# A hybrid encoder layer on one core: recurrence's values loaded by POOL, fill's weights one piece sooner, decays' rows ahead of sums, gates in quarters, factors a step sooner

## The chip, the core and the metric

The kernel runs on one core of one Trainium2 chip. The metric is the device time of one execution in microseconds; three runs of the kernel before gave 1386.80, 1387.91 and 1392.83 us, so its median is 1387.91 us. The engines are PE (matrix products), DVE and ACT (elementwise work), POOL, and SP, which only starts transfers. Transfers can be started by SP, ACT or POOL; each has its own queue, in which a transfer that waits holds the ones behind it.

## What is computed

One layer of a bidirectional encoder on 1024 rows of width 1024, all in float32:

```python
proj = x @ w_in[l]
(aq, ak, av, gq, gk, gv, gout, lr_f, lr_b, gate_a, gate_g) = jnp.split(proj, IN_SPLITS, axis=-1)
for gi, (win, dil) in enumerate(((128,1), (512,4), (2048,16))):      # mixer A, three groups of 4 heads
    o_g, lse_g = _dilated_group(aq[:, :, hs], ak[:, :, hs], av[:, :, hs], bias, dil, k_side)
mix_w = jax.nn.softmax(jnp.stack(lses, axis=0), axis=0)
y_attn = jnp.sum(mix_w[..., None] * jnp.stack(outs, axis=0), axis=0)
...
b = jnp.cumsum(log_a, axis=3)                                        # mixer B, 4 heads, both directions
chunk_kv = jnp.einsum('bhncd,bhncv->nbhdv', k * jnp.exp(b_last - b), v)
_, s_prev = lax.scan(step, jnp.zeros((B, H, dk, dv), jnp.float32), (decay, chunk_kv))
...
y = sigmoid(gate_a) * (y_attn @ w_attn_branch) + sigmoid(gate_g) * (rmsnorm(o_gla) * silu(gout) @ w_gla_branch)
x = LayerNorm(alpha * x + y @ w_out)
x = LayerNorm(alpha * x + (relu(x @ w_ff1 + b_ff1) ** 2) @ w_ff2 + b_ff2)
```

## The kernel before

Each float32 operand of a product is split into a high and a low part (`halve`: ACT casts the high part, DVE subtracts to get the low part), and `mm3` makes three matmuls of each product (L102, L103, L104). The large projections are computed with sums of input and weight blocks, so DVE adds weights before they are used (L213 to L221, `psum`) and adds products afterwards (`add`, L159).

The places that the change touches, in order of time:

- **The decays' rows.** Early in the program `psteps` runs pieces of 12 matmuls whose products DVE sums at L159 into `fu` and `fcr`. Between them `pre1` (L495) needs two small operands on PE: `lrt`, cast and subtracted by DVE (L470, L471), and `wzr` (L466, L467), from `wz`, which POOL loads.
- **The recurrence** (mixer B, heads 0 to 3). `gv`, 2 MB of values, is loaded from the scratch `gvd` in two halves; `kv` (L549) multiplies them with `kt`, which ACT copies (L541); `states` makes `U` and `S` of the products on DVE (L550 to L569), `out` (L592) uses `S`. Between the heads' steps `fill` puts pieces of other projections on PE, each with its weights: `fetch_raw` loads them (SP), `split` makes the halves, `keep` copies the result to `xb` (L629, ACT) and stores it. `extra` says after which fill a weight is loaded and split. `after_raw` hangs each SP load behind the last one, so SP's order is the order of the code.
- **The steps of `proj`.** A step prepares its weights: two loads of `praw` or `pwhi`, sums on DVE, then halves `pwhi`, `pwlo` (L155 on ACT, L156 on DVE), and 12 matmuls follow three steps later. `yT` and `yB`, two copies of 2 MB each that these steps use later on, are loaded from `xsd` by SP.
- **The units.** While the later steps run, a table hangs other work on them, one unit for each step: the tiles of the attention (`att`, eight for each of the three groups, g = 2, 1, 0) and the gates of mixer B. A tile's parts are `scores` (L893 into the PSUM bank `sc`, read by DVE at L899), `turned` (L917), `values` (L932 into `avp`). For g = 0, `weigh` and `shares` make the factors `f` of the three groups on DVE (L977 to L993), `spread` turns them on PE (L999) into the same bank `sc`, ACT copies them to `fT` and stores them to `fdr`, `loadw` loads them spread out (`W<-fdr`, POOL, held until `fdr` has landed), and `mix` (L953 to L962) multiplies on DVE. `at` gives each tile's unit. A gate is a product and a split on DVE (L1066, L156) and an ACT cast.

Tile's scheduler sets the order within an engine where the code does not (`tc.issue_after`, `behind`) say it.

Of the kernel before, what the change touches and what calls it, by code (L numbers as in the profile page):

```python
# [8 lines left out]
F32 = mybir.dt.float32  # L9
# [63 lines left out]
def build(tc, io):  # L73
# [84 lines left out]
    def add(o, a, b):  # L158
        issued["add"] = V.tensor_tensor(o, a, b, op=OP.add)  # L159
# [577 lines left out]
    del issued["add"]  # L737
# [4 lines left out]
    for i in range(2):  # L742
        issued["raw"] = after_raw(SP.dma_start, gv[:, 4 * i:4 * i + 4], gvd[512 * i:512 * i + 512].rearrange("(t p) f -> p t f", p=128))
    xb_t = ring(P.open("tmp", side="right"), [128, 512], F32, 4, "xb")
    stg = P.open("stg", bufs=2, side="right")
    for h, H in enumerate(heads):
# [6 lines left out]
        if h in (1, 2):  # L753
            load_qk(h + 1)
# [5 lines left out]
        fill(1 if h == 1 else 2)  # L760
        step(H["intra"], 1)
# [90 lines left out]
    def att(g, t):  # L852
# [198 lines left out]
    def gate(hs, part=None):  # L1051
        if hs[0] % 2 == 0 and not part:
            yg.append(xp.tile([128, 2, 4, 512], F32R, tag="act", name=f"yg{hs[0]}"))
        if part:
            pass
        elif hs == (0, 1):
            A.activation(yraw[0][:, :, 0], yraw[0][:, :, 0], AF.Silu)
        else:
            for h, sl, t in gates[hs]:
                A.activation(t[:, 0], t[:, 0], AF.Silu)  # L1060
        for h, sl, t in gates[hs] if part is None else gates[hs][part:part + 1]:
            a, n = 2 * (h % 2) + sl.start // 512, (sl.stop - sl.start) // 512
            o = yg[h // 2][:, :, a:a + n]
            g, y = (t[:, i].rearrange("p (a n) -> p a n", a=n) for i in range(2))
            with behind("add"):
# [952 lines left out]
```

## Time and profile before

| | |
|---|---|
| median of three runs | 1387.91 us |
| the profiled execution | 1391.62 us |
| its span, first to last instruction | 1389.8 us |
| PE busy, share of the span | 1358.5 us, 98% |
| DVE, ACT, POOL busy | 74%, 46%, 10% |
| chain that ended last, by engine | PE 84%, DMA 7%, DVE 4%, ACT 2% |
| mean granted clock of PE | 0.988 of full speed |

PE's idle time and the stretches in which its granted clock is below 1.00 are what is left beside the matmuls. A view of waits groups the idle time of an engine by the instruction that waited and by what released it; a timeline gives each instruction with the idle time in front of it.

### The profile page before, as it was taken

Reading aid. Unit: us, or ns where it says so; the run is one execution under the profiler, and the core shown is the slowest. Engines: PE = TensorE matmul, PEld = TensorE weight load, DVE = VectorE, ACT = ScalarE, POOL = GpSimd, SP = SyncE. Lnnn points to the kernel's source line nnn. Section 1 sums busy time; section 2 is a strip of 40 time slices with the busy share of each in tenths; the row PEclk is TensorE's granted clock in tenths of the full one; section 3 lists DMA queues with packets and bytes.
Section 4 is the critical chain, followed back from the end, with each engine's and each line's share of the span. In section 5 each row is a group of like instructions: output and inputs, shape, how many; then the busy total and the mean of one; then the engine's idle time right before and its main releaser. Section 6 shows DMA issues by size and latency. Waiting matters only on the chain.

```text
span 1389.8 us, 19080 instructions
## 1 busy us (share of the span) xinstructions
PE 1358.5 (98%) x6757; PEld 1125.5 (81%) x6757; DVE 1031.9 (74%) x1782; ACT 640.1 (46%) x1200; POOL 142.0 (10%) x226
## 2 busy tenths in 40 slices
PE   9988989999999999999999999999999999999998
PEld 7967888789777777788888888888888888888886
DVE  7766577366777788767666787887867897786988
ACT  7434665321456544244416655555556533333343
POOL 0000222200344433100001000000000000000001
PEclk9998999999999999999999999999999999999999
DMA  8457654765576677765753565666555965445313
GB/s 307 146 167 243 182 170 159 277 206 185 171 254 224 204 212 212 226 209 195 269 205 132 217 215 173 233 212 219 199 210 166 362 221 165 154 130 160 105 31 122
DMA packets 130212, 272.71 MB, mean 196 GB/s; under 512 B 36677, under 2 KB 48293, under 8 KB 129604
## 3 DMA queue, kind: packets, MB, share of 16 engines
q1 hardware_dynamic: 115060, 235.12, 50.9%
q0 software_dynamic: 11488, 34.88, 7.9%
q10 hardware_dynamic: 3568, 1.49, 0.4%
q8 instruction: 53, 0.87, 0.3%
q14 instruction: 43, 0.35, 0.1%
HBM read 185.57 MB, written 89.01 MB: 198 GB/s over the span
## 4 chain that ended last, share of the span: by engine, by line
PE 84%; DMA 7%; DVE 4%; ACT 2%; issue 1%; SPq 1%; POOL 0%; POOLq 0%; ACTq 0%; DVEq 0%
PE ps L102 18%; PE ps L103 18%; PE ps L104 18%; PE mm L102 6%; PE mm L103 6%; PE mm L104 6%; DMA W<-fdr 1%; DMA fdr<-fT 1%; PE sc L104 1%; PE sc L102 1%; PE sc L103 1%; PE avp L932 1%; DMA pwhi<-in_wfm 1%; PE sc L893 1%; PE tr L917 1%
## 5 line engine op out<-in xcount | busy, mean ns | idle before, releaser
L1390 ACT CAST T<-hp 128x1024 fp32r<-128x1024 f32 x36 | 37.9, 1052 | 109.8 <-PE ps L103 70.3
L1896 POOL TENSOR_TENSOR mv<-mv,mhalf 128x1 f32<-128x1 f32 x8 | 7.0, 877 | 607.3 <-DVE mv L1895 605.8
L103 PE MATMUL ps<-B,B 128*128 128x512 f32 x160 | 62.2, 389 | 0.0
L104 PE MATMUL ps<-B,B 128*128 128x512 f32 x160 | 62.2, 389 | 0.0
L102 PE MATMUL ps<-B,B 128*128 128x512 f32 x160 | 60.9, 390 | 0.5 <-ACT B L1390 0.5
L905 ACT ACTIVATE e<-e,sm 128x256 f32<-128x256 f32 (+2 forms) x96 | 43.3, 453 | 31.4 <-DVE sm L899 31.1
L104 PE MATMUL ps<-T,T 128*128 128x512 f32 x144 | 56.0, 389 | 0.0
L103 PE MATMUL ps<-T,T 128*128 128x512 f32 x144 | 56.0, 389 | 0.0
L102 PE MATMUL ps<-B,T 128*128 128x512 f32 x144 | 56.0, 389 | 0.0
L103 PE MATMUL ps<-B,T 128*128 128x512 f32 x144 | 56.0, 389 | 0.0
L104 PE MATMUL ps<-B,T 128*128 128x512 f32 x144 | 56.0, 389 | 0.0
L102 PE MATMUL ps<-T,T 128*128 128x512 f32 x144 | 56.0, 389 | 0.0
L1391 DVE TENSOR_TENSOR T<-hp,T 128x1024 fp32r<-128x1024 f32 x36 | 44.0, 1222 | 15.2 <-ACT T L1390 15.1
L1791 DVE TENSOR_TENSOR acc<-ps,acc 128x512 f32<-128x512 f32 x68 | 45.7, 688 | 12.7 <-PE ps L104 12.2
L102 PE MATMUL mm<-xB,whi 128*128 128x512 f32 x128 | 51.4, 402 | 0.0
L104 PE MATMUL mm<-xB,wlo 128*128 128x512 f32 x128 | 50.5, 394 | 0.0
L103 PE MATMUL mm<-xB,whi 128*128 128x512 f32 x128 | 50.4, 393 | 0.0
L102 PE MATMUL ps<-T,fraw 128*128 128x512 f32 x128 | 49.6, 390 | 0.4 <-ACT T L1390 0.4
L103 PE MATMUL ps<-T,fraw 128*128 128x512 f32 x128 | 49.8, 389 | 0.0
L104 PE MATMUL ps<-T,fraw 128*128 128x512 f32 x128 | 49.6, 389 | 0.0
L1509 ACT ACTIVATE c<-c,cols 128x512 f32<-128x512 f32 x48 | 34.7, 725 | 27.8 <-DVE c L1570 13.1
L159 DVE TENSOR_TENSOR cr<-cu,mm 128x512 f32<-128x512 f32 x45 | 34.5, 766 | 16.7 <-PE mm L104 16.4
(741 smaller groups left out, 4342.5 us busy)
## 6 DMA issues: line engine op xcount, KB each, us to landing
hdr<-c SPq DMA_DIRECT2D x112, 256.0 KB, 2.6
hp<-hdr SPq DMA_DIRECT2D x56, 512.0 KB, 3.8
spill<-cr SPq DMA_DIRECT2D x48, 256.0 KB, 4.6
raw<-in_wfm SPq DMA_DIRECT2D x17, 512.0 KB, 4.0
praw<-in_wfm SPq DMA_DIRECT2D x16, 512.0 KB, 5.5
pwhi<-in_wfm SPq DMA_DIRECT2D x16, 512.0 KB, 5.1
gate<-spill SPq DMA_DIRECT2D x32, 256.0 KB, 3.1
wa<-in_w SPq DMA_DIRECT2D x16, 512.0 KB, 4.8
```

What stands on the lines that cost most here:

```text
L102: T.matmul(ps, lh, rh, start=first and i == 0, stop=False, skip_group_check=more)
L103: T.matmul(ps, lh, rl, start=False, stop=False, skip_group_check=more)
L104: issued["pe"] = T.matmul(ps, ll, rh, start=False, stop=last and i == n - 1, skip_group_check=more)
L159: issued["add"] = V.tensor_tensor(o, a, b, op=OP.add)
L893: mm = T.matmul(sps[i][:, pr, 0:w], q[ps_, pr], k[ps_, pr, 0:w], start=True, stop=True)
L905: issued["exp"] = A.activation(e, e, AF.Exp, bias=sm[:, h:h + 1], scale=-1.0, accum_out=sm[:, 4 + h:5 + h])
L917: T.transpose(tp[0:hi - lo, pr, j], b["e"][i][:, pr, lo:hi], ident)
L932: return T.matmul(av[64 * i:64 * i + 64, pr], vv[:, h * 64:h * 64 + 64], b["et"][i][p0:p0 + vv.shape[0], pr, j], start=j == pr == 0, stop= ...
L1390: A.copy(o[:, 0], src)
L1391: V.tensor_tensor(o[:, 1], src, o[:, 0].bitcast(F32), op=OP.subtract)
L1509: A.activation(q, src, AF.Relu, bias=cols[:, 2 * j + f:2 * j + f + 1])
L1791: V.tensor_tensor(m, p, m, op=OP.add)
```

## The change

It has six parts, none of which changes an arithmetic operation of the result, only order, queues and the size of pieces.

1. `add` issues behind `issued["decay"]`, the last of `lrt`, `wzr`, and these stand first in the code.
2. `gv` is loaded by POOL (`pool_dma`) and not by SP; the raw weights of the fourth fill piece are loaded earlier on SP.
3. Fill weights are loaded one piece sooner; the third of the attention's value weights has a tile of its own (`vr3`) and is loaded and split first; `load_qk` stands behind the fill.
4. The two 2 MB loads from `xsd` stand behind the raw loads of the first three steps.
5. The gates are made in pieces of 512 columns; those of heads 0 and 1 in four units (35, 37, 39, 41).
6. For g = 0, `shares` comes a unit sooner, `spread` stands right behind `turned` (behind "small", not behind "pe"), and the spacing of the tiles changes.

```diff
     def add(o, a, b):
-        issued["add"] = V.tensor_tensor(o, a, b, op=OP.add)
+        with behind("decay"):
+            issued["add"] = V.tensor_tensor(o, a, b, op=OP.add)
...
-            raws[i] = wp.tile([128, 2, 384], F32, tag="raw", bufs=2, name="raw")
+            raws[i] = (gp.tile([128, 2, 384], F32, name="vr3") if i == 3 else
+                       wp.tile([128, 2, 384], F32, tag="raw", bufs=2, name="raw"))
...
-        if p > 2:
-            extra.setdefault(n - 3, []).append(firsts[p][0])
-    for n, f, i in ((5, v_raw, 0), (5, v_raw, 1), (6, v_split, 0), (6, v_split, 1), (6, v_raw, 3), (6, v_raw, 2),
-                    (7, v_split, 3), (7, v_split, 2)):
+    for p in range(4, NP):
+        n = p if p < 8 else p + 4
+        extra.setdefault({12: 6, 13: 7}.get(n, n - 4), []).append(firsts[p][0])
+    for n, f, i in ((2, v_raw, 3), (4, v_raw, 0), (5, v_raw, 1), (6, v_split, 0), (6, v_raw, 2), (6, v_split, 1),
+                    (7, v_split, 2), (7, v_split, 3)):
...
-    issued["raw"] = after_raw(SP.dma_start, gv[:, 4 * i:4 * i + 4], gvd[512 * i:512 * i + 512].rearrange("(t p) f -> p t f", p=128))
+    pool_dma(gv[:, 4 * i:4 * i + 4], gvd[512 * i:512 * i + 512].rearrange("(t p) f -> p t f", p=128))
...
-        after_raw(SP.dma_start, XQ[nm].bitcast(F32), xsd[i])
...
     for i in range(3):
         steps[i][0]()
+    for i, nm in ((1, "T4"), (0, "B22")):
+        with behind("sp"):
+            issued["sp"] = SP.dma_start(XQ[nm].bitcast(F32), xsd[i])
...
-                with tc.issue_after(issued["pe"].ins):
+                with tc.issue_after(issued["small"].ins):
                     issued["small"] = T.transpose(tp, b["f"][:, 0:3].rearrange("p g h -> p (g h)"), ident)
...
-        for n, part in ((i + 1, 0), (i - 2, 3), (i, 1), (i - 2, 8), (i - 1, 2)):
+        for n, part in ((i + 1, 0), (i - 2, 3), (i, 1), (i - 2, 8), (i - 1, 2), (i - 1, 6)):
...
-    at = [n0 + 2 + (i * 2.7 if i < 8 else 19 + (i - 7) * 1.9 if i < 16 else 36.1 + (i - 16) * 2.4) for i in range(26)]
+    at = [n0 + 2 + (i * 2.7 if i < 8 else 19 + (i - 7) * 1.8 if i < 16 else 35.2 + (i - 16) * 2.7) for i in range(26)]
...
-    for hs, a, bs in (((0, 1), 33, (36, 38)), ((2,), 41, (45, 46)), ((3,), 48, (51, 52))):
+    for hs, a, bs in (((0, 1), 32, (35, 37, 39, 41)), ((2,), 43, (47, 49)), ((3,), 50, (53, 55))):
```

On DVE, where the decays' rows are made (`xr` is the relative bias, `fu` and `fcr` are sums of PE's products). Before:

```order
L450 TENSOR_SCALAR xr_136<-sc 12x512
L159 TENSOR_TENSOR fu_114<-fu_114,mm 128x512
L159 TENSOR_TENSOR fcr_116<-fu_114,mm 128x512
L159 TENSOR_TENSOR fcr_116<-fcr_116,mm 128x512
L470 CAST lrt<-tr 96x512 x2
L471 TENSOR_TENSOR lrt<-tr,lrt 32x512 x2
L466 CAST wzr<-wz 96x512
L467 TENSOR_TENSOR wzr<-wz,wzr 32x512
```

And in the changed kernel, same engine and place:

```order
L451 TENSOR_SCALAR xr_136<-sc 12x512
L469 CAST lrt<-tr 96x512 x2
L470 TENSOR_TENSOR lrt<-tr,lrt 32x512 x2
L471 CAST wzr<-wz 96x512
L472 TENSOR_TENSOR wzr<-wz,wzr 32x512
L160 TENSOR_TENSOR fu_114<-fu_114,mm 128x512
L160 TENSOR_TENSOR fcr_116<-fu_114,mm 128x512
L160 TENSOR_TENSOR fcr_116<-fcr_116,mm 128x512
```

The four instructions on `lrt` and `wzr` moved ahead of the three sums.

On SP, between the early spills and the recurrence, `gv` stands behind the last `fcr` spill before:

```order
L624 DMA raw<-in_wfm 128x1024
L204 DMA spill<-fcr_116 128x512
L204 DMA spill<-fcr_117 128x512
L204 DMA spill<-fcr_118 128x512
L624 DMA gv<-gvd 128x4x512 x2
L624 DMA raw<-in_wfm 128x1024
```

On POOL in the changed kernel the load of `gv` is the next transfer after `wz`, ahead of the first `upk` of a fill piece:

```order
L164 DMA wz<-in_wz 96x512
L473 MEMSET rmask 128x1024
L474 MEMSET rmask 64x8
L475 MEMSET rmask 64x8
L164 DMA gv<-gvd 128x4x512 x2
L164 DMA upk<-xb_1095 128x512
```

So `gv` moved from SP's queue to POOL's.

On PE, in a tile of g = 0, the turning of the factors stands after twelve matmuls of a step before (the rows of these matmuls between are left out here by starting at the last two):

```order
L103 MATMUL mm<-xT_96,pwlo 128x512
L104 MATMUL mm<-xT_96,pwlo 128x512
L999 MATMUL sc<-ident,f_2464 12x128
L102 MATMUL mm<-yT_2396,pwlo 128x512
L103 MATMUL mm<-yT_2396,pwlo 128x512
```

In the changed kernel it follows the tile's own scores and transposes at once:

```order
L902 MATMUL sc<-ak_2449,aq_2446 128x256 x4
L926 MATMUL tr<-ident,e_2455 128x128 x4
L926 MATMUL tr<-ident,e_2456 128x128 x4
L1008 MATMUL sc<-ident,f_2464 12x128
L102 MATMUL mm<-xT_96,pwlo 128x512
```

It moved up by twelve matmuls, to right behind `tr`.

## Rows read from the trace of the kernel before

**Rows 1.** The view of waits of PE over the whole span. Columns: the instruction that waited, what released it, us in total, times, longest.

```profile
PE tr L549 <- DMA gv<-gvd: 4.9, 2, 2.9
PE sc L495 <- DVE wzr L467: 4.6, 1, 4.6
PE mm L102 <- ACT xb L629: 3.2, 1, 3.2
PE mm L104 <- DVE pwhi L156: 2.7, 1, 2.7
PE sc L999 <- DVE f L993: 2.3, 3, 1.4
PE mm L102 <- DVE cr L159: 1.5, 2, 1.1
PE sc L102 <- ACT pwlo L155: 1.4, 1, 1.4
PE av L592 <- DVE S L569: 1.3, 1, 1.3
```

**Rows 2.** The view by windows, the five windows of 25 us in which the granted clock is below 1.00. Columns: window, its length, busy us and instructions of PE, PEld, DVE, ACT, POOL, then the mean granted clock, the DMA share, GB/s.

```profile
75.00:100.00 25.00, 20.45 (x76) 16.01 (x76) 17.07 (x21) 10.23 (x15) 0.00 (x0) 0.86 0.40 114
100.00:125.00 25.00, 19.60 (x92) 16.01 (x91) 12.64 (x21) 7.55 (x11) 1.50 (x4) 0.80 0.74 245
...
175.00:200.00 25.00, 21.74 (x136) 20.38 (x137) 16.58 (x20) 12.79 (x39) 6.62 (x10) 0.93 0.60 196
...
275.00:300.00 25.00, 23.35 (x97) 19.03 (x97) 16.90 (x22) 4.58 (x7) 0.73 (x1) 0.93 0.63 184
...
400.00:425.00 25.00, 22.34 (x117) 17.10 (x117) 19.59 (x51) 14.70 (x37) 10.24 (x17) 0.93 0.70 216
```

**Rows 3.** PE's timeline between 80 and 125 us. Columns: start, us, engine, line, operation, out<-in, count, and in brackets the idle time in front of it with its releaser.

```profile
80.46 1.19 PE L495 MATMUL sc<-lrt,wzr 96*128 96x512 f32 x2 [4.55 <-DVE wzr L467]
...
97.74 0.50 PE L102 MATMUL tr<-xB,swlo 128*128 128x512 f32 x1
...
114.72 2.05 PE L549 MATMUL tr<-gv,kt 128*128 128x128 f32 x8 [2.86 <-DMA gv<-gvd]
...
121.46 0.63 PE L102 MATMUL mm<-xB,whi 128*128 128x512 f32 x1
...
124.44 0.39 PE L103 MATMUL mm<-xB,whi 128*128 128x512 f32 x1
124.67 0.40 PE L104 MATMUL mm<-xB,wlo 128*128 128x512 f32 x1
```

**Rows 4.** DVE's timeline between 75 and 98 us, same columns.

```profile
75.94 0.69 DVE L159 TENSOR_TENSOR fcr<-fcr,mm 128x512 f32<-128x512 f32 x1 [2.06 <-PE mm L104]
...
79.63 0.68 DVE L467 TENSOR_TENSOR wzr<-wz,wzr 32x512 fp32r<-32x512 f32 x1
...
89.70 0.69 DVE L159 TENSOR_TENSOR fcr<-fu,mm 128x512 f32<-128x512 f32 x1 [0.72 <-PE mm L104]
...
97.00 0.68 DVE L159 TENSOR_TENSOR fcr<-fu,tr 128x512 f32<-128x512 f32 x1
```

**Rows 5.** The view of transfers between 60 and 125 us, two of its issues. Columns: out<-in, queue, count, KB each, median us from issue to landing. POOL issued `wz` at 65.81.

```profile
gv<-gvd SPq DMA_DIRECT2D x2, 1024.0 KB, 9.7
...
wz<-in_wz POOLq DMA_DIRECT2D x1, 192.0 KB, 7.8
```

**Rows 6.** SP's timeline and POOL's, the issue of `gv` and the next transfer that POOL issues after `wz`.

```profile
108.54 0.99 SPq L624 DMA_DIRECT2D gv<-gvd  x2
...
111.37 1.10 POOL L163 DMA_DIRECT2D upk<-xb  x2 [43.54 <-ACT xb L629]
```

**Rows 7.** ACT's timeline around 111 us.

```profile
110.48 1.07 ACT L629 COPY xb<-mm 128x512 f32<-128x512 f32 x2 [4.24 <-DMA spill<-fcr]
111.44 1.09 ACT L541 COPY kt<-tr 128x512 f32<-128x512 f32 x2
```

**Rows 8.** ACT's timeline at 163 us, and PE's at 189 us.

```profile
163.52 0.84 ACT L155 CAST wv<-raw 128x768 fp32r<-128x768 f32 x1 [4.87 <-DMA raw<-in_wtv]
...
189.03 0.51 PE L102 MATMUL mm<-whi,xB 128*128 128x384 f32 x1 [3.21 <-ACT xb L629]
```

**Rows 9.** SP's timeline, the second weight load of the third step, issued behind the two loads from `xsd`; and DVE's timeline, the sum that waits for it.

```profile
257.80 0.33 SPq L190 DMA_DIRECT2D pwhi<-in_wfm  x1
...
272.07 0.69 DVE L213 TENSOR_TENSOR psum<-pwhi 128x512 f32<-128x512 f32 x1 [5.57 <-DMA pwhi<-in_wfm]
```

**Rows 10.** DVE's timeline at 407 us, a half of a gate and the low half of a step's weights behind it.

```profile
406.62 1.25 DVE L156 TENSOR_TENSOR yg<-yraw,yg 128x1024 fp32r<-128x1024 f32 x1
407.75 0.72 DVE L156 TENSOR_TENSOR pwhi<-praw,pwhi 128x512 fp32r<-128x512 f32 x1
```

**Rows 11.** PE's timeline, the matmul that follows the transposes L917 in two tiles of g = 0.

```profile
496.57 0.48 PE L102 MATMUL mm<-xT,pwhi 128*128 128x512 f32 x1
...
505.47 0.48 PE L102 MATMUL mm<-xT,pwlo 128*128 128x512 f32 x1
```

**Rows 12.** DVE's timeline in the same two tiles, the second of the four readings of the scores, and one product with the loaded factors in a late tile.

```profile
496.20 0.42 DVE L899 CUSTOM_DVE_ANT_0 e<-sc,strip 128x256 f32<-128x256 f32 x1
...
505.87 0.42 DVE L899 CUSTOM_DVE_ANT_0 e<-sc,strip 128x256 f32<-128x256 f32 x1
...
583.69 0.42 DVE L953 TENSOR_TENSOR W<-avp,W 128x256 f32<-128x256 f32 x1 [3.72 <-DMA W<-fdr]
```

More of the change, by code (lines that the diff above doesn't have):

```diff
@@ L465, in build @@
     pool_dma(wz, io["wz"])
-    V.tensor_copy(wzr, wz)
-    V.tensor_tensor(wzr[64:96], wz[64:96], wzr[64:96].bitcast(F32), op=OP.subtract)
     for i in range(2):
@@ L471, in build @@
         V.tensor_tensor(lrt[32:64, sl], lp[i][32:64], lrt[32:64, sl].bitcast(F32), op=OP.subtract)
+    V.tensor_copy(wzr, wz)
+    issued["decay"] = V.tensor_tensor(wzr[64:96], wz[64:96], wzr[64:96].bitcast(F32), op=OP.subtract)
     G.memset(rmask, 1.0)
@@ L694, in build @@
         extra.setdefault(n - 2, []).append(firsts[p][1])
-        if p > 2:
-            extra.setdefault(n - 3, []).append(firsts[p][0])
-    for n, f, i in ((5, v_raw, 0), (5, v_raw, 1), (6, v_split, 0), (6, v_split, 1), (6, v_raw, 3), (6, v_raw, 2),
-                    (7, v_split, 3), (7, v_split, 2)):
+    for p in range(4, NP):
[3 more added lines that the diff above has]
+                    (7, v_split, 2), (7, v_split, 3)):
         extra.setdefault(n, []).append(lambda f=f, i=i: f(i))
+    extra[6].sort(key=lambda f: f is firsts[8][0])
+    extra[7].sort(key=lambda f: f is firsts[9][0])
     count = itertools.count()
@@ L736, in build @@
                 firsts[1][1]()
-    del issued["add"]
+            firsts[3][0]()
+            issued["sp"] = issued["raw"]
+    del issued["add"], issued["decay"]
     issued["raw"] = issued["sp"]
@@ L752, in build @@
         step(H["intra"], 0)
-        if h in (1, 2):
-            load_qk(h + 1)
         step(H["kv"], 0)
@@ L760, in build @@
         fill(1 if h == 1 else 2)
+        if h in (1, 2):
+            load_qk(h + 1)
         step(H["intra"], 1)
@@ L1049, in gate_load, with gate @@
             pool_dma(t[:, 1], yodr[h, :, sl])
-    def gate(hs, part=None):
-        if hs[0] % 2 == 0 and not part:
+    def gate(hs, part):
+        if hs[0] % 2 == 0 and part == 0:
             yg.append(xp.tile([128, 2, 4, 512], F32R, tag="act", name=f"yg{hs[0]}"))
-        if part:
-            pass
-        elif hs == (0, 1):
+        if part == 0 and hs == (0, 1):
             A.activation(yraw[0][:, :, 0], yraw[0][:, :, 0], AF.Silu)
-        else:
+        elif part == 0:
             for h, sl, t in gates[hs]:
                 A.activation(t[:, 0], t[:, 0], AF.Silu)
[L1061 to L1065, printed above, removed]
-                V.tensor_tensor(y, y, g, op=OP.mult)
-                halve(o[:, 0], o[:, 1], y)
+        n = 2 if hs == (0, 1) else 1
+        h, sl, t = gates[hs][part // n]
+        q = part % n
+        g, y = (t[:, i, 512 * q:512 * q + 512] for i in range(2))
+        o = yg[h // 2][:, :, 2 * (h % 2) + sl.start // 512 + q]
+        with behind("add"):
+            V.tensor_tensor(y, y, g, op=OP.mult)
+            halve(o[:, 0], o[:, 1], y)
     vs = ap_.tile([128, 2, 768], F32, tag="strip1", name="vs")
@@ L1157, in build @@
         units.setdefault(n, []).append(lambda i=i: visit(i))
-        for k, part, later in ((i - 1, 6, 1), (i, 4, 1), (i, 5, 2), (i - 1, 7, 1), (i - 2, 9, 1)):
-            if 0 <= k < 24 and (later == 1 or k > 15):
+        for k, part, later in ((i, 4, 1), (i, 5, 1), (i - 1, 7, 1), (i - 2, 9, 1)):
+            if 0 <= k < 24:
                 units.setdefault(n + later, []).append(lambda k=k, part=part: tiles[k][part]())
```

## Prediction, made before the changed kernel ran

> **What bounds the kernel now.** PE does. I read the shares of the engines first: PE is busy nearly throughout, and the chain that ended last is PE for most of its length. So only what shortens PE's stops, or what they do to its clock, can pay; DVE, ACT and the queues count where PE waits for them. Then I read the waits of PE, to see how few there are: eight entries hold 22.4 us [rows 1]. Then the windows of 25 us, to see what a stop costs beyond itself: the granted clock is below 1.00 in five windows only, and each holds one of the long stops [rows 1, 2]. A clock of 1.00 is 2.4 GHz and half of it 1.2 GHz; a mean of c over 25 us means 2 x (1 - c) x 25 us at the low level, and PE loses at most half of that: 3.5, 5.0, and three times 1.75, together 13.75 us [rows 2]. The matmuls confirm the two levels: seven pitches from 121.46 to 124.44 are 0.426 us each, the next is 0.23 [rows 3]. Stops of up to 1.4 us were followed by no such window [rows 1, 2]; 1.4 plus a second of 0.2 just behind it was. So a stop of some 1.6 us or more costs about 1.75 us on top. Last I read the timelines around each stop, to see what ends the wait and what stands next in line.
>
> **Part 1, decays' rows.** PE stopped 4.55 us at 80.46 for `wzr`, which DVE made only after the sum at 75.94, itself held by PE [rows 3, 4]. In the new order the four small instructions stand ahead of the sums. What then holds `wzr` is its load: issued at 65.81, 7.8 us to landing, so 73.6 [rows 5], plus the cast (0.4) and subtraction of 0.68 [rows 4]: 74.7, before PE arrives at 80.46 - 4.55 = 75.9. The stop goes, and with it most of the first window's clock loss: I take 3.0 of the 3.5 [rows 2]. Gain 7.55. The sums now stand behind a load; if it landed 1.2 us later, PE would wait again.
>
> **What is late next.** The decays' chain (ACT, then DVE's scans) starts only 4.55 us earlier plus 0.3 for its own products at full clock. DVE's idle 0.72 at 89.70, a wait for PE, vanishes too [rows 4]. So DVE's sum at 97.00 ends at 97.7 - 5.5 = 92.2, while PE reaches the matmul behind it, which it started at 97.74 with hardly a wait, at 97.74 - 7.55 = 90.2 [rows 3, 4]. A new stop of 2.0 us, at which the clock may fall (half a chance of 1.75 to 2: 1.0). A known stop of 0.5 just behind it, for the next sum, is absorbed.
>
> **Part 2, gv by POOL.** SP issued `gv` at 108.54, behind three spills that wait for their sums; it took 9.7 us [rows 5, 6], and PE stopped twice, 4.9 us in all [rows 1], with up to 5.0 of clock behind it [rows 2]; I take 3.8, since part of that time PE stood still. POOL has nothing to issue for 43 us before 111.37 [rows 6]. In its queue `gv` waits only for the last reader of the memory that it takes, which stands ahead of the matmul at 97.74 [rows 3]. Issued as late as that, moved up with PE to 90.2, it lands at 99.9. PE wants it at 114.72 - 2.86 = 111.86 [rows 3], less 7.55 and the 0.5, plus the new 2.0: 105.8. Slack 5.9 us. Gain 8.7 and the 0.5.
>
> Then the other operand is late: ACT's copies `kt` at 111.44, done at 112.5, stand behind copies that waited 4.24 us for a spill's landing [rows 7]. That chain is DVE's and moves with it, 5.5 us: 107.0 against 105.8, a stop of 1.2 to 1.4, too short for the clock by the rule above. So parts 1 and 2 give 7.55 + 9.2 - 2.0 - 1.0 - 1.4 = 12.4 us; without any new stop 16.8, with the clock falling at both of them and twice the stops about 8.
>
> The POOL rows show the descriptors' price: two issues of 128 rows each take 1.10 us together [rows 6], and each half of `gv` has 512. The Trainium skill speaks against this move: "SBUF — State Buffer", section "SBUF: two separate sides", says that a transfer issued by GpSimd needs that engine to write its descriptors, that it cannot while DVE runs certain two-port operations, and advises to issue from SP or ACT. By that rule the issue would stretch while DVE works at 80 to 90 us; POOL does nothing between 75 and 100 us here [rows 2], so no row shows it. It is a rival below; the slack of 5.9 us is what it must exceed.
>
> **Part 3, fill's weights.** At 163.52 ACT had waited 4.87 us for a load of the value weights, and everything behind it on ACT and DVE, with it `S` and the copies `xb`, was late by that much [rows 8]. PE's stops of 1.3 for `S` and 3.2 for `xb` follow [rows 1, 8], and 1.75 of clock [rows 2]: 6.3 in all. In the new order this weight has memory of its own, is loaded after the third fill, and is split early; the chain of `S` starts when PE's products are there. The later `q` and `k` loads move behind one or two fills, and stay well ahead of their use. I take 5.5: the early cast now stands ahead of keep copies on ACT, and a wait of half a microsecond there is likely. Bounds 3 and 6.3.
>
> **Part 4, xsd.** The load at 257.80 stood behind 4 MB and reached DVE at 272.07 after 14.3 us, where DVE had stood 5.57 us [rows 9]. PE's stop is 1.4 plus 0.2, and 1.75 of clock [rows 1, 2]: 3.35. With the 4 MB behind it, the load takes less; only 1.6 us less is needed. What was ahead is now later: the 4 MB land at worst the same 14.3 us after their issue, about 273, and their first reader stands 36 matmuls (8 us at 0.23) behind the matmul that stopped near 276. About 10 us of cover. I take 3; bounds 1.4 and 3.4.
>
> **Part 5, gates.** DVE's gate halves of 1.25 us stood ahead of a weights' half at 407.75 [rows 10]; PE stopped 2.7 us, and 1.75 of clock [rows 1, 2]: 4.4. In the new order half of the gate's work comes behind these weights, two products and two subtractions of 1.25 us each in halves, that is 2.5 us of DVE work less ahead of them. The 2.7 goes nearly whole; I take 3.5, bounds 1 and 4.4, since quarters in later units may press elsewhere.
>
> **Part 6, factors.** It removes the three waits for `f`, 2.3 us, and likely the two for `cr`, 1.5, since the factors' loads, for which DVE stood 3.72 us at 583.69 [rows 12], start sooner [rows 1]. But the turned factors go into the bank of the scores, and now PE must wait, right behind its transposes, until DVE has read that bank twice. In one tile the second reading ended at 496.62, PE was there at 496.57; in another, 506.29 against 505.47 [rows 11, 12]. So a stop of 0.05 to 0.8 in each of eight tiles. From the new order on DVE I count four with nothing ahead (0.1 each), three with three or four 0.6-us rows ahead (0.4 to 0.5), and the last tile, whose factors themselves end behind six such rows (some 1.7): 3.7. Net 0; bounds -6 (all stops at 0.8, two more at 2 us with a fall of the clock) and +3.5.
>
> **Sum.** 12.4 + 5.5 + 3.0 + 3.5 + 0 = 24.4 us. The profiled execution took 1391.6 (span 1389.8), so 1367 there. It stands 3.7 above the median of the runs shown, which no stop explains; the same stops are in both, so from 1387.9 I forecast **1363 us**.
>
> **The rivals.**
> - The gaps close whole: all bounds at their best, 16.8 + 6.3 + 3.4 + 4.4 + 3.5 = 34.4, so 1353.5. For it: every removed wait has a named cause. Against it: DVE's chain at 97 us moves less than PE. 8%.
> - The chain of DVE takes over: the new stops for `fcr` and `kt` are twice as long and each drops the clock, and part 3 gives 3: 8 + 3 + 3 + 3.5 = 17.5, so 1370. For it: DVE is continuous from 89.7 to 97.7 but for the one wait [rows 4]. 20%.
> - POOL's descriptors: `gv` comes over 5.9 us later than I think and the stop with its clock stays: 8.7 are given back, and the 1.4 for `kt` with them not paid: 24.4 - 7.3 = 17.1, 1371. For it: four times the rows of any issue seen here, while DVE is busy. Against: the issues seen are short [rows 6]. 6%. (The Trainium skill, "SBUF — State Buffer", section "SBUF: two separate sides", is the rule for it.)
> - Slower: the wait for the scores' bank is long in every tile. If DVE has two more rows ahead of the readings, each of eight stops is 0.8 + 1.2 = 2.0, and the clock falls each time, 1.75: 30 us, less the 3.7 counted: 24.4 - 26.3, so 1390; with three rows more, 2.6 + 1.75 each, 1395. It decides from 24.4 / 8 = 3.1 us a tile beyond what I counted. For it: three rows of 0.6 us are enough to get there. Against: four tiles have nothing ahead. 2%.
> - The change does little: the new orders of parts 3 to 6 only move waits, and part 1 and 2 give 8: 1380. 7%.
> - My forecast, 1357 to 1367: 57%.
>
> **How the numbers follow.** 1363 is the likeliest case. The range 1355 to 1377 leaves out most of the first and the last two or three. A measurement of this kernel tells about 0.5% (6.9 us) from no change, so faster means below 1381: forecast, first three rivals and most of the last, 0.94; same 0.04; slower 0.02.
>
> **What would show it.** No waits of PE for `wzr`, `gv`, `pwhi` at 400 us or `xb` at 189; a wait for `fcr` of about 2 us near 90, and for `kt` of 1.4 near 105; `gv` issued by POOL at 80 to 90 and landed 10 us later; windows with a clock below 1.00 only near 90; `sc` at the factors' turning waiting for L908, 0.1 to 0.8 us each, some 1.7 in the last. Wrong would be a stop at `gv`, at the value weights or of over 2 us at each tile.

## The result, and the profile after

The changed kernel takes **1370.24 us** (median of four runs, 1369.64 to 1375.09) where the kernel before takes 1387.36 in the same runs: a ratio of 0.988, 95% interval 0.984 to 0.991. The forecast was 1363, its range 1355 to 1377: right side, inside the range, and 7 us too fast. It lies outside the 1357 to 1367 that the prediction kept for its forecast, on the 1370 of its second rival. The profiled execution took 1369.64 us (span 1367.9).

PE's waits, the longest (columns as in [rows 1]):

```profile
PE sc L1008 <- DVE sm L908: 5.3, 4, 3.8
PE av L102 <- DVE fcr L160: 4.1, 1, 4.1
PE sc L1008 <- DVE f L1002: 1.8, 1, 1.8
PE sc L902 <- DMA ak<-spill: 1.7, 2, 1.3
PE tr L102 <- DVE fcr L160: 1.5, 1, 1.5
...
PE mm L102 <- ACT xb L630: 0.4, 1, 0.4
```

The waits for `gv`, `wzr`, `pwhi`, `pwlo` and `S` of [rows 1] are gone, and that for `xb` has shrunk from 3.2 to 0.4 us. The longest of the new ones are 5.3 us for the bank of the scores (`sm` L908) and 4.1 for `fcr`; the wait for `ak`, 0.4 us before, is 1.7 now and stood in no term of the prediction. Windows of 25 us, columns as in [rows 2]:

```profile
75.00:100.00 25.00, 19.39 (x79) 14.96 (x79) 16.92 (x19) 10.91 (x15) 1.55 (x2) 0.95 0.77 217
100.00:125.00 25.00, 25.00 (x127) 20.50 (x128) 16.53 (x28) 13.04 (x17) 2.06 (x5) 0.92 0.61 189
175.00:200.00 25.00, 25.00 (x169) 23.07 (x168) 20.18 (x31) 15.85 (x25) 6.74 (x14) 1.00 0.67 209
275.00:300.00 25.00, 25.00 (x142) 24.42 (x141) 17.75 (x24) 8.12 (x12) 2.17 (x3) 1.00 0.70 222
400.00:425.00 25.00, 24.55 (x158) 19.25 (x157) 18.86 (x52) 15.74 (x40) 11.57 (x18) 1.00 0.75 248
525.00:550.00 25.00, 20.76 (x114) 16.10 (x114) 20.43 (x66) 9.29 (x28) 7.50 (x13) 0.93 0.70 184
```

Three of the five clock losses of [rows 2] are gone and two are smaller; the one at 525 us is new. Now the place of the 4.1 us, first DVE and PE by their timelines:

```profile
73.43 0.68 DVE L472 TENSOR_TENSOR wzr<-wz,wzr 32x512 fp32r<-32x512 f32 x1
...
96.46 1.23 DVE L530 TENSOR_TENSOR k<-k,ex 128x1024 f32<-128x1024 f32 x1 [5.34 <-DMA k<-spill]
97.60 0.68 DVE L160 TENSOR_TENSOR fcr<-fcr,av 128x512 f32<-128x512 f32 x1
```

```profile
98.34 0.79 PE L102 MATMUL av<-xB,swlo 128*128 128x512 f32 x1 [4.10 <-DVE fcr L160]
98.93 0.63 PE L103 MATMUL av<-xB,swlo 128*128 128x512 f32 x1
...
104.05 0.43 PE L103 MATMUL mm<-xB,whi 128*128 128x512 f32 x1
```

The name behind PE's wait is a sum that takes 0.68 us; DVE's row ahead of it shows the cause: `k<-k,ex` stood 5.34 us for the landing of `k`, and the sum stood behind it. From 98.93 to 104.05 there are 12 pitches of 0.427 us, the low clock, where 0.23 is the full one [rows 3]: 2.4 us more. Now POOL's timeline, and the view of transfers between 60 and 112 us (columns as in [rows 5]):

```profile
78.98 0.79 POOL L164 DMA_DIRECT2D gv<-gvd  x1 [11.81 <-PE mm L104]
85.42 0.76 POOL L164 DMA_DIRECT2D gv<-gvd  x1 [5.66 <-issue]
```

```profile
gv<-gvd POOLq DMA_DIRECT2D x2, 1024.0 KB, 6.2
...
q<-spill SPq DMA_DIRECT2D x4, 256.0 KB, 9.0
k<-spill SPq DMA_DIRECT2D x4, 256.0 KB, 8.0
```

The second half of `gv` goes out at 85.42, when the first has landed, and moves beside SP's `q` and `k` (issued from 86.38 on), of which `q` took 5.1 us before and takes 9.0 now. In windows of 5 us the DMA share, the last column but one, is above 1 in these ten microseconds:

```profile
90.00:95.00 5.00, 3.06 (x12) 2.18 (x12) 1.13 (x2) 3.48 (x5) 0.00 (x0) 1.00 1.05 251
95.00:100.00 5.00, 1.66 (x4) 1.37 (x5) 3.54 (x4) 0.00 (x0) 0.00 (x0) 0.73 1.06 229
```

The other stop is in a tile of g = 0 (DVE's and PE's timelines; between the two DVE rows stand, among others, eleven rows of 0.68 us, sums and weights of the steps of `proj`):

```profile
519.46 0.42 DVE L962 TENSOR_TENSOR W<-avp,W 128x256 f32<-128x256 f32 x1 [2.91 <-DMA W<-fdr]
...
529.86 0.42 DVE L908 CUSTOM_DVE_ANT_0 e<-sc,strip 128x256 f32<-128x256 f32 x1
```

```profile
530.68 0.30 PE L1008 MATMUL sc<-ident,f 128*12 128x128 f32 x1 [3.77 <-DVE sm L908]
```

DVE had waited 2.91 us for the factors to come back from memory, then worked off the rows that had gathered, and only then read the scores. PE had ended its transposes at 526.9. In the eight tiles of g = 0 PE waited, in order, 0, 0.19, 0, 0.83, 0, 3.77 and 0.47 us for the bank, and in the last 1.76 us for the factors `f` themselves.

### The profile page after: what moved, and what is told of

It reads as the page before. It is cut to its first block, busy times and chain, and to the rows that moved or that the text cites. A ratio compares the mean times of both kernels' runs of the same rounds, so it can differ in the third digit from the quotient of the medians.

```text
span 1367.9 us, 19100 instructions
## 1 busy us (share of the span) xinstructions
PE 1346.4 (98%) x6757; PEld 1119.6 (82%) x6757; DVE 1033.7 (76%) x1786; ACT 637.6 (47%) x1200; POOL 143.5 (10%) x228
## 4 chain that ended last, share of the span: by engine, by line
PE 59%; DVE 1%; ACT 1%; DMA 1%; issue 0%; POOL 0%; ACTq 0%; DVEq 0%; POOLq 0%
PE ps L102 18%; PE ps L103 18%; PE ps L104 18%; PE mm L102 1%; PE mm L103 1%; PE mm L104 1%; ACT xr L1417 1%; DMA W<-fdr 0%; PE ps L1414 0%; DMA fdr<-fT 0%; PE ps L1925 0%; DVE cr L160 0%; DVE W L970 0%; PE ps L1921 0%; ACT T L1398 0%
## 5 line engine op out<-in xcount | busy, mean ns | idle before, releaser
L1398 ACT CAST B<-hp 128x1024 fp32r<-128x1024 f32 x20 | 21.0, 1052 | 55.4 <-PE ps L103 48.1
```

Source lines behind the costliest of these rows:

```text
L1398: A.copy(o[:, 0], src)
```

## The experiments

Two theories stood at the start. A: the 24.4 us on record were missed because of part 6, whose waits for the scores' bank give back more than was counted. B: `gv` on POOL takes the transfers that `k` needs, and makes the 4.10 us stop. The rival to each: DVE is late anyway, and the lateness moves on to the next thing whatever is undone.

Each was run against the kernel before again (1385.7 to 1386.5 us in these runs). A price "by medians" is against the changed kernel's 1370.24, which rests on four runs; its ratio's interval is 5 us wide to either side, so of those prices only the order of size counts. Prices "in the stretch" are read from the traces: PE's time from one of these marks to the next, the first product with `S` of head 0, the first scores (`sc<-ak,aq`), and the first product of `T` and `fraw`, behind the attention. In the changed kernel these three rows are:

```profile
131.65 0.39 PE L593 MATMUL av<-S,q 128*128 128x128 f32 x2
...
325.48 0.72 PE L902 MATMUL sc<-ak,aq 64*128 64x128 f32 x8
...
758.80 0.74 PE L102 MATMUL ps<-T,fraw 128*128 128x512 f32 x2 [0.41 <-ACT T L1398]
```

How far such a price can be trusted is shown by the stretches that an edit did not touch. From `S` to the first scores the ten profiles with parts 3 and 4 lie between 193.81 and 193.90 us. From there to `T` the eight with parts 5 and 6 lie between 433.23 and 435.86. Up to `S` one profile, in which only part 5 was undone, is 4.9 us longer than the changed kernel's. So a difference of 2 or 3 us ahead of `S` or behind the first scores, read from one profile, may be that of two executions.

**The kernel before, a second profile.** No edit.

> The kernel before as it is, for a second profile. Theory P (its first profiled execution, 1391.62 where the median is 1387, lost more clock than a usual one, and the terms worked out from it are too large by that): the second profile is nearer 1387, with the same stops within 1 us and a granted clock above 0.988. Rival (all of its executions have that clock, and a profiled one is always some 4 us longer): about 1391 again at 0.988, and the stops of the first.

1385.78 us, median of 12; its profiled execution took 1386.75 (span 1384.9, clock 0.990), 4.9 us less than the first. The same marks, and the stop at 275 us:

```profile
140.03 0.39 PE L592 MATMUL av<-S,q 128*128 128x128 f32 x2
...
275.20 0.50 PE L102 MATMUL sc<-xT,pwlo 128*128 128x512 f32 x1 [1.43 <-ACT pwlo L155]
276.15 0.50 PE L104 MATMUL sc<-xT,pwlo 128*128 128x512 f32 x1 [0.21 <-DVE pwlo L156]
...
342.07 0.71 PE L893 MATMUL sc<-ak,aq 64*128 64x128 f32 x8
...
774.12 0.74 PE L102 MATMUL ps<-T,fraw 128*128 128x512 f32 x2 [0.41 <-ACT T L1390]
```

```profile
275.00:300.00 25.00, 24.59 (x114) 20.92 (x115) 17.86 (x23) 5.07 (x9) 0.73 (x1) 1.00 0.72 213
```

Theory P holds. The stop of 1.43 and 0.21 us is the same as in the first profile, to the hundredth, and this time no low clock followed it (1.00 here, 0.93 in [rows 2]): 1.75 us. The waits for `cr` were 0.3 us here and 1.5 in [rows 1]: 1.2.

**gv on SP again** (part 2 undone for `gv` alone).

```diff
-    pool_dma(gv[:, 4 * i:4 * i + 4], gvd[512 * i:512 * i + 512].rearrange("(t p) f -> p t f", p=128))
+    issued["raw"] = after_raw(SP.dma_start, gv[:, 4 * i:4 * i + 4], gvd[512 * i:512 * i + 512].rearrange("(t p) f -> p t f", p=128))
```

> The changed kernel with gv loaded by SP again, behind the last spills. Theory B, gv's 2 MB on POOL's queue delay the k loads that DVE waits for: k lands 3 us or more sooner, the 4.1 us wait for fcr falls to 1 or less with its low clock (about 2), and the waits for gv come back with their clock (8.7): 1370 + 8.7 - 6 = 1373. Rival, k is late for its own issue: the wait for fcr stays at 4 and 1379.

1375.69 us (ratio 0.990 to 0.993), 2.7 above theory B's sum. DVE's and PE's timelines:

```profile
92.85 1.23 DVE L530 TENSOR_TENSOR k<-k,ex 128x1024 f32<-128x1024 f32 x1 [1.81 <-DMA k<-spill]
```

```profile
94.73 0.50 PE L102 MATMUL av<-xB,swlo 128*128 128x512 f32 x1 [0.58 <-DVE fcr L160]
...
108.44 1.13 PE L550 MATMUL tr<-gv,kt 128*128 128x128 f32 x8 [3.20 <-DMA gv<-gvd]
```

With `gv` out of the way `k` is there 3.6 us sooner and the 4.10 us are 0.58. So `gv` made `k` late, and theory B holds for the stop. In return `gv`'s own two stops are 3.20 and 3.28 us, 6.5 in all and more than the 4.9 of [rows 1]. Part 2 is worth 2.6 us in its stretch, 5.4 by medians.

**gv on POOL, but only once k's factor is made** (one column of `ex` copied into `gv`, so that its load waits).

```diff
     for i in range(2):
+        G.tensor_copy(gv[:, 4 * i, 0:1], qk["ex", 0][:, 0:1])
+    for i in range(2):
         pool_dma(gv[:, 4 * i:4 * i + 4], gvd[512 * i:512 * i + 512].rearrange("(t p) f -> p t f", p=128))
```

> The changed kernel with gv still on POOL, but held until ACT has made ex (near 92 us), by a copy of one column of ex into gv that the load then overwrites. Theory B: k lands near 94 and the wait for fcr falls from 4.1 to about 1 with its low clock; gv still comes in time or under 1.5 us late: 1365 to 1367. Rival, k is late anyway: the wait for fcr stays at 4 and gv is late as well, 1371 to 1375.

1374.05 us, in the rival's range and not in theory B's. POOL's and PE's timelines:

```profile
92.94 0.79 POOL L164 DMA_DIRECT2D gv<-gvd  x1 [0.46 <-DMA k<-spill]
102.48 0.77 POOL L164 DMA_DIRECT2D gv<-gvd  x1 [8.74 <-DMA spill<-fcr]
```

```profile
107.83 2.05 PE L551 MATMUL tr<-gv,kt 128*128 128x128 f32 x8 [2.28 <-issue]
```

The stop for `fcr` fell to 0.82 us, as theory B has it, and two others came instead: 2.28 us at 107.83 and 1.92 at 111.80. Only the second is `gv`'s. At the first, the first half of `gv` had landed long before (92.94 and 9.2 us); what came just ahead of PE's row is ACT's copy `kt` at 107.13, behind a copy that had waited for raw weights. Again the second half of `gv` went out only when the first had landed (9.2 us here).

**The sum ahead of k's product** on DVE.

```diff
-            V.tensor_tensor(qk["k", h], qk["k", h], ex, op=OP.mult)
+            kx = lambda: V.tensor_tensor(qk["k", h], qk["k", h], ex, op=OP.mult)
+            if h:
+                kx()
...
+        if n == 7:
+            with tc.issue_after(issued["add"].ins):
+                for f in qk["late"]:
+                    f()
```

(`late` holds the products of `k` and `q` of head 0.)

> Only edit against the changed kernel: head 0's product k*ex stands one row later on VectorE, behind the sum of fcr and av instead of ahead of it; loads and queues stay. Theory B (the 4.10 us stop of TensorE at 98.34 is k's late landing, passed on only because the sum stands behind the product that waits for k): the stop falls to 0.5 to 1.0 and the granted clock of 95 to 105 us stays near full, so 3.2 us of stop and some 2 us of clock go: 1365 by the changed kernel's 1370.2. Rival (k itself is what is late, and the next thing that needs it takes the stop over): a stop of 2 to 4 us at the transposes of k or at the next sum, 1369 to 1371.

1372.58 us (1369.55 to 1375.65). DVE's, SP's, ACT's and PE's timelines:

```profile
99.03 1.22 DVE L95 TENSOR_TENSOR wlo<-raw,whi 128x1024 fp32r<-128x1024 f32 x1
```

```profile
100.28 0.33 SPq L631 DMA_DIRECT2D raw<-in_wfm  x1
```

```profile
106.27 1.04 ACT L93 CAST whi<-raw 128x1024 fp32r<-128x1024 f32 x1 [3.00 <-DMA raw<-in_wfm]
```

```profile
109.23 3.78 PE L556 MATMUL tr<-gv,kt 128*128 128x128 f32 x16 [4.39 <-ACT kt L548]
```

My theory fell. The 4.10 us stop went entirely, and a 4.39 us stop for `kt` came 11 us later: ACT's copies `kt` stand behind a cast that waits for raw weights. These are late because `k` is: SP issued their load at 100.28, just as DVE's row `wlo`, which reads the weights loaded before, had ended (99.03 and 1.22 us), and `wlo` stands behind the product of `k` at 96.75, which had waited 4.98 us for `k`. In the changed kernel the two rows stand at 99.34 and 100.58, as late, but there PE had already stood still at the sum. So `k`'s lateness is handed on to whatever stands behind its product, as the rival has it. The mark at `S` stands at 132.14, 0.5 us later than in the changed kernel.

**k first on SP**, head 1's `q` and `k` behind the raw weights.

```diff
-        for nm, base in (("q", 0), ("k", 2)):
+        for nm, base in (("k", 2), ("q", 0)):
...
-            for h in range(2):
-                load_qk(h)
+            load_qk(0)
             firsts[2][0]()
...
             firsts[3][0]()
+            load_qk(1)
```

> Only edit against the changed kernel: k goes out ahead of q on SP, and head 1's q and k (1 MB) stand behind the raw weights and not ahead of them. Theory B (k is late because the second half of gv and 2 MB of q and k share the transfer engines from 86 to 97 us): k goes out 1.3 us sooner and shares with less, so the product k*ex starts at 93 to 94.5 and not 96.46; TensorE's 4.10 us stop for fcr falls to 1 to 2.5, the raw weights land sooner too, and no stop takes its place: 1365 to 1367 by the changed kernel's 1370.2. Rival (what is late moves on, as it did when the sum was put ahead of the product): the first stop shrinks and TensorE stops 2 us or more at kt, gv or the next weights: 1369 to 1372.

1375.61 us (1372.11 to 1376.4), 3.6 above even the rival's upper end. ACT's and PE's timelines:

```profile
110.92 1.07 ACT L630 COPY xb<-mm 128x512 f32<-128x512 f32 x2 [4.66 <-DMA spill<-fcr]
```

```profile
98.10 0.50 PE L102 MATMUL av<-xB,swlo 128*128 128x512 f32 x1 [2.81 <-DVE fcr L160]
...
112.54 3.62 PE L550 MATMUL tr<-gv,kt 128*128 128x128 f32 x16 [2.40 <-ACT kt L542]
```

`k` went out 0.9 us sooner than in the changed kernel (86.81), but its product began only 0.24 us sooner (96.22). The first stop shrank by 1.3 us and `kt` stopped PE for 2.40: head 1's loads now stood ahead of two spills of `fcr` on SP, for whose landing the copies `xb` wait, and `kt` stands behind these. `S` is 2.7 us later than in the changed kernel. Whatever went first, something of this stretch came late.

**Part 1 undone** (`lrt`, `wzr` behind the sums; the core of it).

```diff
     def add(o, a, b):
-        with behind("decay"):
-            issued["add"] = V.tensor_tensor(o, a, b, op=OP.add)
+        issued["add"] = V.tensor_tensor(o, a, b, op=OP.add)
```

> The changed kernel with part 1 put back (the rows of lrt and wzr behind the sums). By the prediction's terms, 7.55 less the 2.0 and 1.0 that it counted for what is late next, part 1 is worth 4.5: 1374.7, with a stop of 4.5 us for wzr near 80 us and no 4.10 us stop for fcr. Rival (the 4.10 stop behind it, which is a transfer's, stays as long as it is, because gv's loads move with TensorE): 1377 to 1378.

1378.4 us (1376.24 to 1379.92). PE's timeline:

```profile
105.24 0.79 PE L102 MATMUL av<-xB,swlo 128*128 128x512 f32 x1 [5.65 <-DVE fcr L159]
```

The stop of 4.55 us for `wzr` is back, at 80.16, and the rival is right: the stop for `fcr` stays, and is longer. So it was not PE's earlier arrival that made it, as the prediction had it. Part 1 is worth 6.9 us in its stretch.

**Part 3 undone** (the fill's weights, `vr3` and the place of `load_qk` as before; the core of it).

```diff
-            raws[i] = (gp.tile([128, 2, 384], F32, name="vr3") if i == 3 else
-                       wp.tile([128, 2, 384], F32, tag="raw", bufs=2, name="raw"))
+            raws[i] = wp.tile([128, 2, 384], F32, tag="raw", bufs=2, name="raw")
...
+        if p > 2:
+            extra.setdefault(n - 3, []).append(firsts[p][0])
```

> The changed kernel with part 3 put back (the fill's weights, the third value weight's own tile and the places of the later q and k loads as before). By the prediction's term 5.5: 1375.7, with stops for xb and S back near 150 and 180 us. Rival (its bounds, 3 and 6.3 us): 1373 or 1376.5.

1381.4 us (median of 12), more than either said. In its stretch the price is 5.2 us (the marks are 133.06, 332.13 and 766.22), the term on record being 5.5. The stops of [rows 1] return, that for `xb` at half its length (PE's timeline):

```profile
167.09 0.61 PE L593 MATMUL av<-S,q 128*128 128x128 f32 x2 [1.36 <-DVE S L570]
...
181.06 0.45 PE L102 MATMUL mm<-whi,xB 128*128 128x384 f32 x1 [1.80 <-ACT xb L630]
```

Of the rest, 1.4 us lie ahead of `S`, 0.8 between the first scores and `T`, and 1.3 behind `T`; the profiled execution took 1378.41 us, the least of the twelve. Why the others are longer was not settled.

**Part 4 undone.**

```diff
+        after_raw(SP.dma_start, XQ[nm].bitcast(F32), xsd[i])
...
-    for i, nm in ((1, "T4"), (0, "B22")):
-        with behind("sp"):
-            issued["sp"] = SP.dma_start(XQ[nm].bitcast(F32), xsd[i])
```

> The changed kernel with part 4 put back (the two rows of xsd that the decays need go out ahead of the raw loads again, from where they were). By the prediction's term part 4 is worth 3.0 us: 1373. Rival (the stop it removes returns elsewhere, as it did for part 6): 1370 to 1371.

1373.73 us (1373.39 to 1374.83), as the term on record has it: 3.5 more by medians, 1.85 us in the stretch from `S` to the first scores. The stop is back, 1.29 and 0.21 us at 261.14 and 262.08 for `pwlo`, and no low clock followed.

**Part 5 undone** (gates in halves again; the table of their units).

```diff
-    for hs, a, bs in (((0, 1), 32, (35, 37, 39, 41)), ((2,), 43, (47, 49)), ((3,), 50, (53, 55))):
+    for hs, a, bs in (((0, 1), 33, (36, 38)), ((2,), 41, (45, 46)), ((3,), 48, (51, 52))):
```

> The changed kernel with part 5 put back (the gates in halves, at their old places in the list). By the prediction's term part 5 is worth 3.5 us, stops at the gates of 2 us and more return between 365 and 420 us: 1373.7. Rival (most of the old stop was not the gates' size): 1370 to 1371.

1376.57 us (1371.71 to 1381.73), above both forecasts; the profiled execution took 1381.4 and is 6.0 us longer from the first scores to `T`. PE's timeline:

```profile
395.81 0.70 PE L104 MATMUL mm<-xT,pwhi 128*128 128x512 f32 x1 [2.67 <-DVE pwhi L156]
```

The order of [rows 10] is back (at 392.03 and 393.16), and the stop of 2.7 us of [rows 1], with a clock of 0.93 from 375 to 400 us, and 1.5 and 0.4 us more for `et` besides; PE no longer waits for `ak`. Not all of the 6.0 us is the part's: behind the stop for the scores' bank, 3.53 us here and 3.77 in the changed kernel, the clock from 525 to 550 us was 0.86 and not 0.93, which is 1.75. That leaves some 4.2.

Up to `S`, which this edit does not touch, the same execution lost 4.9 us more than the changed kernel's (136.58 against 131.65). DVE's and PE's timelines:

```profile
75.15 0.42 DVE L471 CAST wzr<-wz 96x512 fp32r<-96x512 f32 x1 [4.83 <-DMA wz<-in_wz]
```

```profile
103.13 0.79 PE L102 MATMUL av<-xB,swlo 128*128 128x512 f32 x1 [6.75 <-DVE fcr L160]
```

`wz`, issued at 65.47, took 9.7 us to land, where it took 7.8 in the changed kernel. PE waited 0.88 us for `wzr` and 0.70 for a sum, its clock was 0.85 and 0.81 in the two windows of 5 us from 75 on, and the stop for `fcr` was 6.75 us. It is what the prediction warned of in part 1, sums that stand behind a load.

**Part 6 undone**, and **only its turning put back**.

```diff
-                with tc.issue_after(issued["small"].ins):
+                with tc.issue_after(issued["pe"].ins):
...
-        for n, part in ((i + 1, 0), (i - 2, 3), (i, 1), (i - 2, 8), (i - 1, 2), (i - 1, 6)):
+        for n, part in ((i + 1, 0), (i - 2, 3), (i, 1), (i - 2, 8), (i - 1, 2)):
...
-    at = [n0 + 2 + (i * 2.7 if i < 8 else 19 + (i - 7) * 1.8 if i < 16 else 35.2 + (i - 16) * 2.7) for i in range(26)]
+    at = [n0 + 2 + (i * 2.7 if i < 8 else 19 + (i - 7) * 1.9 if i < 16 else 36.1 + (i - 16) * 2.4) for i in range(26)]
```

(The whole part has this and the unit of `shares` as before; its turning alone leaves `at` as changed.)

> The changed kernel with part 6 alone undone (spacing of the tiles, shares and spread as before). Theory A, part 6 costs more than it gives: the waits of PE for L908 (5.3 us) and for f in the last tile (1.8) go, and the low clock at 525 to 550 (1.75) with them; the waits for f (2.3) and for cr (1.5) of the kernel before come back: 5.0 us less than the changed kernel, near 1365. Rival, DVE is late there whatever PE waits for: within 1 us of 1370.

> The changed kernel with only the turning of the factors put back behind the next step (the spacing of the tiles and the sooner shares stay). Theory A, it is the bank of the scores that PE waits for: no wait for L908, at most 1 us for f, so 6 to 8 us less than the changed kernel, 1362 to 1364. Rival, DVE's lateness moves on to the next thing that PE needs: a wait for f or cr of as much, 1368 to 1371.

1368.21 and 1368.79 us, both with a ratio of 0.985 to 0.988; theory A had 1365 and 1362 to 1364. PE's waits without part 6:

```profile
PE av L102 <- DVE fcr L160: 4.6, 1, 4.6
PE sc L902 <- DMA ak<-spill: 2.4, 1, 2.4
PE mm L102 <- DVE cr L160: 1.7, 2, 1.4
...
PE sc L1008 <- DVE f L1002: 1.2, 3, 0.7
```

The 5.3 us for the scores' bank are gone, and the waits for `cr` and `f` are back with 2.9 us, which is less. The 2.4 us for `ak` are no return: every version with part 5 has 1.7 to 2.9 of them. In its stretch part 6 costs 2.5 us by this profile, which also lost 1.75 us of clock from 375 to 425 us (0.94 and 0.99), at the stop for `ak`, where the changed kernel's lost none. By medians it costs 2, which these two kernels alone don't tell from nothing. With the turning alone put back PE still waits 1.7 us for the bank and 2.6 for `f`, where theory A had none and at most 1: for that kernel the rival's range holds.

**k first and part 6 undone**, the two edits together.

> k_first_on_SP with part 6 undone as well. If the two add (4 us for k by theory B, 2 us for part 6 by the medians of the run without it): 1364. If the rival of k_first_on_SP holds: 1368. It would be the fastest version so far in either case, by little.

1367.26 us (1363.18 to 1370.1), ratio 0.985 to 0.989: the lowest median of all, but within the spread of the version without part 6 alone. Its marks are 134.16, 327.97 and 756.88: 2.5 us worse than the changed kernel up to `S`, 4.4 better from the first scores to `T`. Against `k_first_on_SP`, from which it differs by part 6 alone, it is 8.35 us faster, and the runs of the two don't overlap (1372.11 to 1376.4 there); from the first scores to `T` it is 6.3 us faster, of which 1.75 are clock that `k_first_on_SP` lost from 375 to 425 us (0.98 and 0.95). Without the falls of the clock at `ak` the two pairs agree, 4.2 and 4.6 us. So part 6 does cost, near the 5 us of theory A. The forecast of 1364 rested on `k`, which brought nothing.

## Why the prediction came out 7 us short

The measured time is that of the second rival, 1370, to which the prediction gave 20%, but by chance. Of that rival's items the stops for `fcr` came, more than twice as long as forecast and with a fall of the clock; no stop for `kt` came, part 3 gave what was taken for it, and part 6 lost what the rival left at nothing. (By its own items that rival's 8 us for parts 1 and 2 would be some 6.5, and its time 1372.)

The ledger, from the marks (us from one to the next; the gain is the second profile of before less the changed kernel):

| stretch | before, first | before, second | changed | gain | on record |
|---|---|---|---|---|---|
| to the first product with `S` | 140.75 | 140.03 | 131.65 | 8.4 | 12.4 (parts 1, 2) |
| to the first scores | 204.35 | 202.04 | 193.83 | 8.2 | 8.5 (parts 3, 4) |
| to `T` | 433.67 | 432.05 | 433.32 | -1.3 | 3.5 (parts 5, 6) |
| to the end of the span | 611.0 | 610.8 | 609.1 | 1.7 | 0 |
| sum | 1389.8 | 1384.9 | 1367.9 | 17.0 | 24.4 |

- **What bounds the kernel**: right. PE is still 98% of the span, and each gain and loss is a stop of PE or its clock.
- **Part 1**: right in its removal, which brings 6.9 us by one profile. The load of `wz` landed in time, DVE's second row on `wzr` began at 73.43 and PE did not stop there; in the profile with part 5 undone it landed later, and PE did.
- **What is late next**: this step failed: "A new stop of 2.0 us" and "A known stop of 0.5 just behind it, for the next sum, is absorbed." The first was 1.51; the second, called absorbed, was 4.10, and cost 2.4 of clock. Stops and clock are 8.0 us where 2.0, 1.0 and 1.4 for `kt` stood, 3.6 of the 4.0 us missing in this stretch (3.3 against the first profile, from which the terms were read). The step followed DVE and PE, and left `k` where it was: `k`'s landing was in none of the rows read, and in no term.
- **Part 2**: `gv` itself was in time, its slack held. What was wrong is that its transfer had no price. The stretch in which `q` and `k` move was full before it came: in the kernel before, the DMA share is 1.05 from 95 to 100 us and 1.01 from 100 to 105. In the changed kernel 1 MB of `gv` stands there as well, and the share is no higher. Neither moving the product (`k_behind_sum`), nor `k` (`k_first_on_SP`), nor `gv` (`gv_after_ex`, `u2_gv_on_SP`) took anything away in sum: the mark at `S` stands at 132.14, 134.35, 134.05 and 134.23 in these, 131.65 in the changed kernel. The differences are smaller than the 4.9 us by which the same code differed up to `S`, so they show that none gained and not which is worst. That `gv` makes `k` late is shown (theory B), and in `k_behind_sum` what hands it on is the order of DVE. That no order in this stretch could gain, because the traffic as such fills it, is argued from the four and from the share; a kernel that loads less there was not run.
- **The descriptors' rival** did not come: POOL's two issues of 512 rows took 0.79 and 0.76 us, not four times the 0.55 of those of 128 rows [rows 6], and landed 6.1 and 6.4 us later. The second did so while DVE was busy for 4.92 of the 5 us from 85 to 90. The Trainium skill, "SBUF — State Buffer", section "SBUF: two separate sides", has it that GpSimd can't write descriptors during some of DVE's operations; the trace shows no such stretching here. Whether any of DVE's rows in these 5 us is such an operation is not shown.
- **Parts 3 and 4**: right, 8.2 against 8.5; undone one by one they are worth 5.2 and 1.85 in the stretch. Part 4's 3.0 held 1.75 for a clock that falls in one execution of the kernel before and not in another.
- **Part 5**: right within its bounds: 6.0 in the stretch, of which 1.75 is clock at another part's stop, so some 4.2 where 3.5 stood. Undone, it also brought 1.9 us of waits for `et`, of which the two profiles of before had 0.4 and 1.1. What it costs is the wait for `ak`, 1.28 us at 395.00 and 0.45 at 411.75 in the changed kernel, which is absent with part 5 undone; how the gates bring it was not looked into.
- **Part 6**: net 0 on record, -2.5 and -6.3 measured, -4.2 and -4.6 without the clock lost at `ak`. The mechanism was the one named (DVE's rows ahead of the readings), and seven of the eight tiles came as counted: 3.25 us in all, with 1.76 in the last where 1.7 stood. (The prediction's own items for all eight add up to 3.3 to 3.6, not 3.7.) The term failed in the sixth tile: 3.77 us with a clock of 0.93 behind it, 1.75 more, where at most 0.5 stood. DVE was late there from a wait for `W`, and rows counted in an order say nothing of a wait ahead of them.
- **The profiled execution against the median**: "3.7 above the median, which no stop explains" was right about stops and left out what does: low clocks that follow the same stop in one execution and not in the next, and `cr`. With that falls the rule behind the terms of clock, that "a stop of some 1.6 us or more costs about 1.75 us on top": stops of 1.51 and 1.76 us in the changed kernel cost none. (The eight entries of [rows 1] add up to 21.9 us, not 22.4.) Against that execution the changed kernel's own is 22.0 us shorter, 2.4 less than the sum; against the second, and by the medians, 17. So the gap is largely that the sum was made against an execution with more lost than usual (1.75 and 1.2 us of it named above).
- The gain of 1.7 us behind `T`, where nothing was changed, is of this kind too: the last group of four matmuls (`ps<-acc,dg`) took 1.98 us in the changed kernel's profile and 3.41 in the second of before, and all fourteen profiles lie between 609.0 and 611.0 us there. It is no term of the change. That group lies in a sixth window below 1.00, the last of the span (0.84 in the first profile of before), which [rows 2] leaves out.

Open: the parts undone one by one cost 6.9, 2.6, 5.2, 1.85, 6.0 and -2.5 in their own stretches, 20.0 us, which lies with the 20.0 to `T` by the first profile of before and above the 15.3 by the second. Each is from one profile and, but for parts 3 and 4, no surer than the 2.6 to 4.9 us seen in stretches that no edit touched. By medians they add up to 32.6 (8.2, 5.4, 11.2, 3.5, 6.3 and -2.0), about twice the whole. Each of these holds the changed kernel's median of four runs, so 3 us in it would be 18 in the sum; how much of the excess that is, and how much is parts set to each other, was not settled, since the changed kernel was not timed again and no part was run alone on the kernel before.

## What to carry to other kernels

A load moved to a queue that is idle is not free: look at the DMA share of the stretch into which it moves, and at what else is in flight there, above all loads that nobody waits for yet. When a wait goes, ask not only which engine is late next but which transfer, and put its landing among the rows. And price a part in its own stretch, between two marks of the bound engine, before trusting medians that differ by a few us; profiles in which that stretch was left alone tell how far the price can be trusted.

## What the runs showed of the hardware

- PE's clock after a stop is not settled by the stop's length alone. The same 1.43 and 0.21 us were followed by a low clock in one execution of the kernel before and not in another. With part 5 undone 0.88 and 0.70 us at 76.44 and 77.84 were followed by 0.85 and 0.81 in the windows of 5 us from 75 on. Stops of 1.51 and 1.76 us (changed kernel) had none at once behind them, nor had 1.87 at 398 us with part 4 undone; 2.93 us at 97.62 in `k_first_no_part_6` had none until 110 us, while 2.81 us at 98.10 in `k_first_on_SP` was followed by 0.88 and 0.78 in the next windows of 5 us.
- The second of two 1 MB loads on POOL's queue went out only when the first had landed: 5.66 us of idle time between the issues in the changed kernel, 5.65 in `k_first_on_SP`, 8.74 in `gv_after_ex` where the landing took longer. In these three the issue comes 0.3 us behind the landing (in the changed kernel 78.98 and 6.1 us, then 85.42). The two issues of 128 rows of [rows 6] follow each other at once. SP's `gv` of [rows 6] has no such pause. What holds the second load was not found: the profile names no wait for it.
